# Linear attention in a mixer with experts: scores of two levels side by side in TensorE's order

## The chip, the cores and the metric

One core of a Trainium2 chip. The time is the device time of one execution in microseconds (us); several executions are run and their median is given. The profile shows one execution instruction by instruction. Its engines are TensorE (PE, with PEld for the loading of weights), VectorE (DVE), ScalarE (ACT), GpSimd (POOL) and SyncE (SP), which issues most DMAs.

## The reference

The layer takes x of 1024 tokens by 1024 features. It projects it by w_in into four HGRN heads of 128 and four GLA heads (keys of 64, values of 128), runs gated linear attention over each head, normalises each head, gates it, multiplies by w_out, and then goes through a layer norm, a hierarchical mixture of 64 experts (two a token) and another layer norm. The attention, cut to what matters:

```python
b = jnp.cumsum(lg, axis=3)                         # log decay
decay = jnp.exp(where(causal, b[t] - b[s], -inf))
scores = einsum('tk,sk->ts', q * decay, k)
o_intra = einsum('ts,sv->tv', scores, v)
S_next = exp(b_last) * S + einsum('sk,sv->kv', k * exp(b_last - b), v)
o = o_intra + einsum('tk,kv->tv', q * exp(b), S)
```

## The kernel before

The mixer runs until about 470 us of the profile; the experts follow. Everything of the mixer on TensorE is written in the order in which it shall run (`manual_schedule` for PE); for VectorE, ScalarE, GpSimd and SyncE a scheduler sets the order from the recorded program.

The work is cut into projections and six units. The projections (L174) multiply x with columns of w_in, in 48 matmuls a block (two halves of the tokens, eight slices of the features, three terms of a split of both factors into a high and a low part). `weights` loads a block's weights in two halves, ScalarE rounds them (L153) and VectorE takes the rest (L154). `fill(n)` issues the next n projections, `need(i)` those up to block i.

Units 0 to 3 are one HGRN head each (`nh = 1`), units 4 and 5 two GLA heads each (`nh = 2`). `gla(u, ...)` does a unit. The causal scores inside a chunk of 128 tokens are made in seven levels, li = 0 to 6: level 0 holds pairs of neighbours, level li the pairs between two blocks of 2^li. `level(li)` (L440) makes the scaled keys and queries: GpSimd subtracts decays (L462, L465), ScalarE takes the exponent (L463, L466), VectorE multiplies (L464 for keys Kb, L467 for queries Qb); for level 0 it is ScalarE twice (L451, L452) and VectorE four times (L453 to L456). There are two buffers each of Kb, Qb and d. `scores(li)` (L470) issues a burst of small matmuls into a PSUM bank, L477 for levels 0 to 4, L492 for 5, L504 for 6; levels 0 to 4 are then merged into `acc` by VectorE (`masked`, L428 and L431) and copied into A by GpSimd at level 4 (L484), levels 5 and 6 are copied into A by ScalarE (L497, L506). `banks` takes a bank of the pool "trp" for the first head, of "ou" for the second.

The loop over levels stands between projections: twelve of them before each burst (`n_lv`), at most one turn in front of a burst. Turns are transposes: those in `before` bring the output of the unit before into rows (L615, VectorE's copy L616), `turn_k` does the decayed keys (L538, ScalarE's copy L539). `decayed_k` and `decayed_q` make the keys and queries for the states.

Then the state phase of the unit: `state(0)` (L572, VectorE's copy L577), and for each of eight chunks the product of queries with the last state (L588), the product of A with values (L590), the next state (L572, VectorE L579), ScalarE's squares (L597), VectorE's copy (L598), and 12 projections (6 in unit 5). Among the chunks `prepare(u + 1)` runs: a logarithm (L379), one operation on k (L381), eight scans that make P, the running sum of the log decay (L400).

Of the kernel before, what the change touches and what calls it, by code (L numbers as in the profile page):

```python
# [9 lines left out]
F32 = mybir.dt.float32  # L10
# [10 lines left out]
NT = T // 128  # L21
# [35 lines left out]
def mixer_moe_kernel(ctx: ExitStack, tc: tile.TileContext, x_in, xT_in, wf_in, wv_in, wvg_in, wa2_in,  # L57
# [48 lines left out]
    ps_sc = ps_tr  # L106
# [89 lines left out]
    def fill(n):  # L196
        end = count[0] + n
        while count[0] < end and step():
            pass
# [204 lines left out]
    def gla(u, n_0, n_lv, n_ch, before, during):  # L404
# [26 lines left out]
                    V.copy_predicated(second(acc[:, hh], li), m.to_broadcast([128, NT, 16 >> li, 1 << li]),  # L431
                                      sps[hh].rearrange("p c (n h) -> p c n h", h=1 << li))

        def banks(shape):

            n = shape[0] * shape[1]
            return [(ps_sc.tile([128, 512], F32, name="trp") if hh == 0 else ps_ou.tile([128, 512], F32, name="ou"))
                    [:, :n].rearrange("p (c t) -> p c t", c=shape[0]) for hh in range(nh)]

        def level(li):  # L440
            h = 1 << li
            Kt, Qt = Kb[flip[0]], Qb[flip[0]]
            flip[0] ^= 1
            v4 = lambda a: a.rearrange("p (b two h) -> p b two h", two=2, h=max(h, 1))
            Kv, Qv, qv, kv, Pv = v4(Kt), v4(Qt), v4(q), v4(k), v4(P)

            if li == 0:
                lo_ = lg.rearrange("p (b two) -> p b two", two=2)[:, :, 1]
                e = g2.tile([128, T], F32, name="d")
                ep, em = e[:, :512, None], e[:, 512:, None]  # L450
                S.activation(ep[:, :, 0], lo_, AF.Exp, scale=0.5 * sc)  # L451
                S.activation(em[:, :, 0], lo_, AF.Exp, scale=-0.5 * sc)  # L452
                V.tensor_tensor(Qv[:, :, 0], qv[:, :, 0], em, OP.mult)  # L453
                V.tensor_tensor(Qv[:, :, 1], qv[:, :, 1], ep, OP.mult)
                V.tensor_tensor(Kv[:, :, 0], kv[:, :, 0], ep, OP.mult)
                V.tensor_tensor(Kv[:, :, 1], kv[:, :, 1], em, OP.mult)  # L456
            else:
                nb = T // (2 * h)
                e = g2.tile([128, T], F32, name="d")
                ev = v4(e)  # L460
                ref = Pv[:, :, 0, h - 1:h].to_broadcast([128, nb, h])
                G.tensor_tensor(ev[:, :, 0], ref, Pv[:, :, 0], OP.subtract)  # L462
                S.activation(ev[:, :, 0], ev[:, :, 0], AF.Exp, scale=sc)  # L463
                V.tensor_tensor(Kv[:, :, 0], kv[:, :, 0], ev[:, :, 0], OP.mult)  # L464
                G.tensor_tensor(ev[:, :, 1], Pv[:, :, 1], ref, OP.subtract)  # L465
                S.activation(ev[:, :, 1], ev[:, :, 1], AF.Exp, scale=sc)  # L466
                V.tensor_tensor(Qv[:, :, 1], qv[:, :, 1], ev[:, :, 1], OP.mult)  # L467
            return Kt, Qt

        def scores(li, Kt, Qt):  # L470
            if li < 5:
                sp = banks([NT, 16 if li else 32])
                for c in range(NT):
                    for hh in range(nh):
                        for j in range(4):
                            o = c * 128 + 32 * j
                            PE.matmul(sp[hh][32 * j:32 * j + 32, c], Kt[rows[hh], o:o + 32],  # L477
                                      second(Qt[rows[hh], None, o:o + 32], li)[:, 0], start=True, stop=True)
                masked(sp, li)
                if li == 4:  # L480
                    for hh in range(nh):
                        for j in range(4):
                            d_ = slice(32 * j, 32 * j + 32)
                            (G.tensor_copy if hh == 0 else S.copy)(A[hh][d_, :, d_], acc[d_, hh])  # L484
            elif li == 5:
                sp = banks([4, 32])
                for c in range(NT):
                    for hh in range(nh):
                        for b in range(2):
                            o = c * 128 + 64 * b  # L490
                            u_ = 64 * b + 32 * (c % 2)
                            PE.matmul(sp[hh][u_:u_ + 32, c // 2], Kt[rows[hh], o:o + 32],  # L492
                                      Qt[rows[hh], o + 32:o + 64], start=True, stop=True)
                for hh in range(nh):
                    for b in range(2):
                        for e in range(2):
                            S.copy(A[hh][64 * b:64 * b + 32, e::2, 64 * b + 32:64 * b + 64],  # L497
                                   sp[hh][64 * b + 32 * e:64 * b + 32 * e + 32])
            elif nh == 1:
                sp = ps_sc.tile([128, 4, 64], F32, name="trp")  # L500
                for c in range(NT):
                    o = c * 128
                    u_ = 64 * (c % 2)
                    PE.matmul(sp[u_:u_ + 64, c // 2], Kt[:, o:o + 64], Qt[:, o + 64:o + 128], start=True, stop=True)  # L504
                for e in range(2):
                    S.copy(A[0][0:64, e::2, 64:128], sp[64 * e:64 * e + 64])  # L506
            else:
                sp = banks([NT, 64])
                for c in range(NT):
                    o = c * 128  # L510
                    for hh in range(nh):
                        PE.matmul(sp[hh][rows[hh], c], Kt[rows[hh], o:o + 64], Qt[rows[hh], o + 64:o + 128], start=True,
                                  stop=True)
                for hh in range(nh):
                    S.copy(A[hh][0:64, :, 64:128], sp[hh][rows[hh]])
# [6 lines left out]
        def decayed_q():  # L522
            S.activation(QI, P, AF.Exp, scale=sc)
            V.tensor_copy(gdec, QI.rearrange("p (c i) -> p c i", i=128)[:, :, 127])
            V.tensor_tensor(QI, q, QI, OP.mult)

        def decayed_k():
            d = dd[0] = g1.tile([128, T], F32, name="lg")
            G.tensor_tensor(d.rearrange("p (c i) -> p c i", i=128), Pc[:, :, 127:128].to_broadcast([128, NT, 128]),
                            Pc, OP.subtract)  # L530
            S.activation(d, d, AF.Exp, scale=sc)
            V.tensor_tensor(d, k, d, OP.mult)

        def turn_k(half):
# [3 lines left out]
                PE.transpose(tp[:, i], dd[0][:, c * 128:(c + 1) * 128], ident)  # L538
            S.copy(KLt[:, half * 4:half * 4 + 4], tp)  # L539

        kqs = {0: level(0)}
        fill(n_0)
        for li in range(7):
            if li < 6:
                kqs[li + 1] = level(li + 1)
            if li == 2:
                decayed_k()
            if li == 3:
                decayed_q()
            fill(n_lv)  # L550
            if before and li > 1:
                before.pop(0)()
            if li in (5, 6):
                turn_k(li - 5)
            scores(li, *kqs.pop(li))
        fill(n_lv)


# [875 lines left out]
```

## Time and profile before

| | |
|---|---|
| runs | 1562.93, 1564.44, 1565.14 us, median 1564.44 us |
| profiled execution | 1563.61 us, its span 1561.8 us |
| busy share: PE, DVE, ACT, POOL | 92%, 45%, 29%, 25% |
| mean granted TensorE clock | 0.992 of full speed |

A row of the timeline gives the start and the length of an instruction (or of several alike), its engine, line, tiles and shapes; in brackets stands how long the engine was idle just before and what released it. Matmuls are pipelined: their ends are modelled, and the distance of starts tells the pace. The rows on which the prediction rests follow the change.

### The profile page before, as it was taken

To read this page: it belongs to the slowest core of one execution; us is meant where nothing else is said; L and a number is where in the kernel's file an instruction comes from. 1 tells how busy PE (TensorE), PEld (TensorE's weight loads), DVE (VectorE), ACT (ScalarE), POOL (GpSimd) and SP (SyncE) were. 2 spreads that over 40 slices of the span, in tenths; PEclk is the share of its full clock that TensorE was granted. 3 is DMA by queue.
4 is the path that set the end of the run, shared out by engine and by line. 5 is a ranking of instruction groups with operands and counts; after the bars stand their busy time and mean duration, and the time that the engine had idled before them with its cause. 6 is when DMAs were issued, how large, how long until landed. Compare 5 with 4: busy or idle time off the path is not lost. (4 is left out here: it accounts for less than half of the span.)

```text
span 1561.8 us, 23129 instructions
## 1 busy us (share of the span) xinstructions
PE 1437.8 (92%) x9359; PEld 800.1 (51%) x9359; DVE 707.6 (45%) x1719; ACT 451.1 (29%) x921; POOL 385.7 (25%) x281
## 2 busy tenths in 40 slices
PE   8899999899999999999998999999999899899895
PEld 5687787777788883333343333333344333334331
DVE  5666655647563783425234224223423333233224
ACT  5556555455531432121211111111121111111210
POOL 2524322423102211322212211321222122112211
PEclk9999999999999999999999999999999999999998
DMA  4111011100048349999999999999999999999992
GB/s 164 49 34 35 29 42 36 34 29 29 29 149 321 125 176 392 423 425 426 426 425 426 426 426 424 427 425 426 427 426 427 425 427 426 426 426 425 426 375 89
DMA packets 63311, 449.15 MB, mean 288 GB/s; under 512 B 12256, under 2 KB 20704, under 8 KB 38880
## 3 DMA queue, kind: packets, MB, share of 16 engines
q1 hardware_dynamic: 52032, 430.27, 66.4%
q0 software_dynamic: 9216, 12.61, 2.2%
q10 hardware_dynamic: 1952, 4.75, 0.8%
q8 instruction: 75, 1.23, 0.3%
q14 instruction: 36, 0.29, 0.1%
HBM read 447.58 MB, written 20.97 MB: 300 GB/s over the span
## 5 line engine op out<-in xcount | busy, mean ns | idle before, releaser
L1183 PE MATMUL gu<-w2u,VOA 128*64 128x512 f32 x992 | 338.9, 595 | 28.0 <-DMA w2u<-in_wg_dram 16.5
L1183 PE MATMUL gu<-w1u,VOA 128*64 128x512 f32 x1040 | 344.3, 595 | 15.0 <-DMA w1u<-in_wg_dram 14.9
L1183 PEld LDWEIGHTS gu<-w2u,VOA 128*64 128x64 f32 x992 | 101.7, 137 | 208.0 <-issue 154.2
L1045 ACT ACTIVATE VOA<-tp,cols 128x128 f32<-128x128 f32 x256 | 96.3, 457 | 337.0 <-PE tp L1042 336.7
L1032 POOL DMA_INDIRECT out_dram<-VOA,oidx x32 | 32.3, 1010 | 601.9 <-DVE VOA L1084 586.3
L1214 PE MATMUL yp<-w1u,hT 128*64 128x512 f32 x496 | 169.8, 599 | 12.1 <-DVE hT L1062 11.8
L1214 PE MATMUL yp<-w2u,hT 128*64 128x512 f32 x496 | 170.0, 598 | 11.7 <-DVE hT L1062 11.7
L1183 PEld LDWEIGHTS gu<-w1u,VOA 128*64 128x64 f32 x1040 | 106.5, 137 | 143.5 <-issue 108.8
L174 PE MATMUL pp<-xh,wh 128*128 128x512 f32 x416 | 172.9, 416 | 0.1
L174 PE MATMUL pp<-xh,wl 128*128 128x512 f32 x416 | 165.0, 397 | 1.9 <-DVE wl L154 1.9
L174 PE MATMUL pp<-xl,wh 128*128 128x512 f32 x416 | 166.4, 400 | 0.0
L1144 DVE SCALAR_TENSOR_TENSOR VOA<-VOA,cp 128x512 f32<-128x512 f32 x62 | 41.6, 682 | 268.7 <-PE cp L1135 263.4
L1069 DVE SCALAR_TENSOR_TENSOR y<-yp,gcol,y 128x512 fp32r<-128x512 f32 x64 | 47.9, 750 | 237.2 <-ACT y L1068 237.1
L1068 ACT ACTIVATE y<-yp,gcol 128x512 fp32r<-128x512 f32 x64 | 43.9, 687 | 211.2 <-PE yp L1214 208.7
L462 POOL TENSOR_TENSOR d<-P 128x512 f32<-128x512 f32 x36 | 51.3, 1425 | 177.9 <-DVE ny L88 65.3
L1189 ACT ACTIVATE sg<-gu 128x512 f32<-128x512 f32 x32 | 19.2, 599 | 250.6 <-PE gu L1183 250.6
L174 PEld LDWEIGHTS pp<-xh,wl 128*128 128x128 f32 x416 | 79.0, 190 | 19.7 <-DVE wl L154 2.8
L174 PEld LDWEIGHTS pp<-xh,wh 128*128 128x128 f32 x416 | 79.1, 190 | 18.7 <-issue 1.7
L1214 PEld LDWEIGHTS yp<-w1u,hT 128*64 128x64 f32 x496 | 49.0, 136 | 73.4 <-issue 55.3
L174 PEld LDWEIGHTS pp<-xl,wh 128*128 128x128 f32 x416 | 79.2, 190 | 13.8
L1214 PEld LDWEIGHTS yp<-w2u,hT 128*64 128x64 f32 x496 | 51.8, 136 | 63.7 <-issue 45.6
L1135 PE MATMUL cp<-y,same 128*128 128x512 f32 x304 | 78.8, 404 | 0.0
(294 smaller groups left out, 2138.8 us busy)
## 6 DMA issues: line engine op xcount, KB each, us to landing
w1u<-in_wg_dram SPq DMA_DIRECT2D x32, 2048.0 KB, 28.2
w2u<-in_wu_dram SPq DMA_DIRECT2D x31, 2048.0 KB, 30.8
w1u<-in_wu_dram SPq DMA_DIRECT2D x30, 2048.0 KB, 30.1
w2u<-in_wg_dram SPq DMA_DIRECT2D x30, 2048.0 KB, 28.0
w1u<-in_wd_dram SPq DMA_DIRECT2D x30, 2048.0 KB, 29.3
w2u<-in_wd_dram SPq DMA_DIRECT2D x30, 2048.0 KB, 29.5
wr<-in_wf_dram SPq DMA_DIRECT2D x36, 256.0 KB, 2.6
raw<-in_wout_dram SPq DMA_DIRECT2D x16, 256.0 KB, 5.1
```

What stands on the lines that cost most here:

```text
L174: PE.matmul(ps, w[:, k], x_[:, k, ts], start=(k == 0 and j == 0), stop=(k == KT - 1 and j == len(terms) - 1))
L462: G.tensor_tensor(ev[:, :, 0], ref, Pv[:, :, 0], OP.subtract)
L1032: return G.indirect_dma_start(out=dst, out_offset=bass.IndirectOffsetOnAxis(ap=idx, axis=0), in_=src, in_offset=None, bounds_check=rows - ...
L1045: S.activation(xt[:, c], tp[:, i], AF.Identity, bias=cols[:, 42 + c:43 + c], scale=cols[:, 34 + c:35 + c])
L1068: S.mul(yh[:, ns], yps[n], gate_col)
L1069: V.scalar_tensor_tensor(yl[:, ns], yps[n], gate_col, yh[:, ns], op0=OP.mult, op1=OP.subtract)
L1135: PE.matmul(cps[n], m, ys[q][:, i, n * 512:(n + 1) * 512], start=(first and j == 0 and i == 0), stop=(last and j == len(ms) - 1 and i == 1))
L1144: V.scalar_tensor_tensor(xg[:, ns], xg[:, ns], ALPHA, cps[n], op0=OP.mult, op1=OP.add)
L1183: PE.matmul(dst[64 * b:64 * b + 64], xt[:, c, 64 * b:64 * b + 64], utile[6 * p + u + b][:, c], start=(c == 0), stop=(c == KT - 1))
L1189: S.activation(sg, gp, AF.Silu)
L1214: PE.matmul(yps[n][64 * b:64 * b + 64], hT[:, c, 64 * b:64 * b + 64], utile[6 * p + 4 + b][:, c, n * 512:(n + 1) * 512], start=(c == 0), s ...
```

## The change

In the loop over levels, level 0 is still by itself; levels 1 and 2, 3 and 4, 5 and 6 are issued back to back, with 24 projections in front of each pair. Turns no longer stand in front of a burst: those of a pair are spread evenly among its 24 projections. The keys and queries of the two levels of the next pair are made right after a pair's scores are issued, followed by the decayed keys or the decayed queries. So that both bursts of a pair find a bank, in units with one head even levels now take a bank of "ou" and odd ones of "trp"; units with two heads use one of each for every level, as before. The number of projections and all other instructions of TensorE stay. Behind the changed lines the line numbers grow, first by 1, from the state phase on by 10.

```diff
--- before.py
+++ after.py
@@ -431,10 +431,11 @@
                     V.copy_predicated(second(acc[:, hh], li), m.to_broadcast([128, NT, 16 >> li, 1 << li]),
                                       sps[hh].rearrange("p c (n h) -> p c n h", h=1 << li))
 
-        def banks(shape):
+        def banks(shape, li):
 
             n = shape[0] * shape[1]
-            return [(ps_sc.tile([128, 512], F32, name="trp") if hh == 0 else ps_ou.tile([128, 512], F32, name="ou"))
+            trp = lambda hh: hh == 0 and (nh == 2 or li % 2)
+            return [(ps_sc.tile([128, 512], F32, name="trp") if trp(hh) else ps_ou.tile([128, 512], F32, name="ou"))
                     [:, :n].rearrange("p (c t) -> p c t", c=shape[0]) for hh in range(nh)]
 
         def level(li):
@@ -469,7 +470,7 @@
 
         def scores(li, Kt, Qt):
             if li < 5:
-                sp = banks([NT, 16 if li else 32])
+                sp = banks([NT, 16 if li else 32], li)
                 for c in range(NT):
                     for hh in range(nh):
                         for j in range(4):
@@ -483,7 +484,7 @@
                             d_ = slice(32 * j, 32 * j + 32)
                             (G.tensor_copy if hh == 0 else S.copy)(A[hh][d_, :, d_], acc[d_, hh])
             elif li == 5:
-                sp = banks([4, 32])
+                sp = banks([4, 32], li)
                 for c in range(NT):
                     for hh in range(nh):
                         for b in range(2):
@@ -497,7 +498,7 @@
                             S.copy(A[hh][64 * b:64 * b + 32, e::2, 64 * b + 32:64 * b + 64],
                                    sp[hh][64 * b + 32 * e:64 * b + 32 * e + 32])
             elif nh == 1:
-                sp = ps_sc.tile([128, 4, 64], F32, name="trp")
+                sp, = banks([4, 64], li)
                 for c in range(NT):
                     o = c * 128
                     u_ = 64 * (c % 2)
@@ -505,7 +506,7 @@
                 for e in range(2):
                     S.copy(A[0][0:64, e::2, 64:128], sp[64 * e:64 * e + 64])
             else:
-                sp = banks([NT, 64])
+                sp = banks([NT, 64], li)
                 for c in range(NT):
                     o = c * 128
                     for hh in range(nh):
@@ -538,21 +539,30 @@
                 PE.transpose(tp[:, i], dd[0][:, c * 128:(c + 1) * 128], ident)
             S.copy(KLt[:, half * 4:half * 4 + 4], tp)
 
+
         kqs = {0: level(0)}
         fill(n_0)
-        for li in range(7):
-            if li < 6:
-                kqs[li + 1] = level(li + 1)
-            if li == 2:
-                decayed_k()
-            if li == 3:
-                decayed_q()
-            fill(n_lv)
-            if before and li > 1:
-                before.pop(0)()
-            if li in (5, 6):
-                turn_k(li - 5)
-            scores(li, *kqs.pop(li))
+        kqs[1] = level(1)
+        fill(n_lv)
+        scores(0, *kqs.pop(0))
+        kqs[2] = level(2)
+        fill(2 * n_lv)
+        for li in (1, 3, 5):
+            if li > 1:
+                turns_ = [before.pop(0) for _ in range(2) if before]
+                if li == 5:
+                    turns_ += [lambda h=h: turn_k(h) for h in range(2)]
+                n = 2 * n_lv // (len(turns_) + 1)
+                for t_ in turns_:
+                    fill(n)
+                    t_()
+                fill(2 * n_lv - n * len(turns_))
+            for l_ in (li, li + 1):
+                scores(l_, *kqs.pop(l_))
+            if li < 5:
+                for l_ in (li + 2, li + 3):
+                    kqs[l_] = level(l_)
+                (decayed_k if li == 1 else decayed_q)()
         fill(n_lv)
```

The scheduler's order on the other engines moves too. VectorE, from unit 0 to unit 1, before (k, P and Kb, Qb are of unit 1, Sg the states of unit 0, osb its output, wl the rest of projection weights):

```order
L381 TENSOR_SCALAR k<-k 128x1024
L400 SCALAR_TENSOR_TENSOR P<-ones,lg 128x128 x8
L577 COPY Sg_117<-ou 128x128
L154 TENSOR_TENSOR wl<-wr,wh 128x512
L579 SCALAR_TENSOR_TENSOR Sg_118<-Sg_117,gdec,ou 128x128
L453 TENSOR_TENSOR Qb_114<-q,d 128x512
L454 TENSOR_TENSOR Qb_114<-q,d 128x512
L598 COPY osb<-ou 128x128
L455 TENSOR_TENSOR Kb_112<-k,d 128x512
```

And now:

```order
L381 TENSOR_SCALAR k<-k 128x1024
L400 SCALAR_TENSOR_TENSOR P<-ones,lg 128x128 x8
L456 TENSOR_TENSOR Kb_112<-k,d 128x512
L457 TENSOR_TENSOR Kb_112<-k,d 128x512
L465 TENSOR_TENSOR Kb_111<-k,d 128x256x2
L587 COPY Sg_117<-ou 128x128
L154 TENSOR_TENSOR wl<-wr,wh 128x512
L589 SCALAR_TENSOR_TENSOR Sg_118<-Sg_117,gdec,ou 128x128
L454 TENSOR_TENSOR Qb_114<-q,d 128x512
```

The three products of unit 1's keys, levels 0 and 1 (L456, L457, L465 of the changed kernel), come ahead of the copy of unit 0's first state (L587), which stood right behind the scans. From unit 1 to 2 it is the same.

ScalarE at the same place, before (KLt are the turned keys, Ab is A, lg the log decay of unit 1, d its exponents):

```order
L539 COPY KLt<-trp 128x512
L497 COPY Ab_115<-trp 32x4x32 x4
L539 COPY KLt<-trp 128x512
L379 ACT_TABLE_LOAD
L379 ACTIVATE lg<-k 128x1024
L506 COPY Ab_115<-trp 64x4x64 x2
L451 ACT_TABLE_LOAD
L451 ACTIVATE d<-lg 128x512
L452 ACTIVATE d<-lg 128x512
```

And now:

```order
L540 COPY KLt<-trp 128x512
L251 ACTIVATE q<-pp 128x512
L540 COPY KLt<-trp 128x512
L379 ACT_TABLE_LOAD
L379 ACTIVATE lg<-k 128x1024
L452 ACT_TABLE_LOAD
L452 ACTIVATE d<-lg 128x512
L453 ACTIVATE d<-lg 128x512
L498 COPY Ab_115<-trp 32x4x32 x4
L507 COPY Ab_115<-ou 64x4x64 x2
```

The table and the two exponents of unit 1's level 0 (L452, L453) come ahead of the six copies of levels 5 and 6 into A (L498, L507), of which four stood ahead of the second copy of the turned keys and two right behind the logarithm. From unit 1 to 2 it is the same.

## Rows read from the trace of the kernel before

**Rows 1.** Waits of TensorE, 40 to 480 us (line waited for: us in all, times, longest).

```profile
PE trp L477 <- DVE acc L431: 3.1, 1, 3.1
...
PE trp L492 <- DVE VOA L616: 1.7, 1, 1.7
PE trp L492 <- DVE acc L431: 1.6, 1, 1.6
PE trp L477 <- DVE acc L428: 1.3, 1, 1.3
```

**Rows 2.** Windows: busy us (x) of each engine, PEclk, DMA share, GB/s.

```profile
700.00:1561.00 861.00, 773.00 (x3303) 311.12 (x3299) 298.59 (x684) 139.94 (x307) 191.00 (x111) 0.99 0.97 409
```

**Rows 3.** Timeline of TensorE about scores 2 of unit 0 (start us, us).

```profile
61.80 0.39 PE L174 MATMUL pp<-xh,wl 128*128 128x512 f32 x1
62.12 0.73 PE L477 MATMUL trp<-Qb,Kb 128*32 128x16 f32 x64
62.78 0.50 PE L174 MATMUL pp<-xh,wh 128*128 128x512 f32 x1
63.12 0.39 PE L174 MATMUL pp<-xl,wh 128*128 128x512 f32 x1
```

**Rows 4.** Timeline of TensorE: a turn that stands alone.

```profile
55.43 0.60 PE L217 MATMUL trp<-cst,vt 128*128 128x128 f32 x4
55.78 0.48 PE L174 MATMUL pp<-xl,wh 128*128 128x512 f32 x1
```

**Rows 5.** Granted clock: two windows, and the matmuls with waits ahead of them.

```profile
339.20:346.00 6.80, 6.80 (x16) 4.90 (x17) 2.24 (x6) 6.01 (x9) 1.01 (x1) 0.50 0.20 69
...
390.40:393.90 3.50, 3.50 (x95) 2.89 (x84) 3.50 (x7) 1.26 (x2) 2.21 (x3) 0.51 0.02 5
...
339.14 1.12 PE L390 MATMUL pp<-gaT,wa 32*128 32x256 f32 x2 [1.13 <-DVE lg L392]
...
389.88 0.22 PE L477 MATMUL trp<-Qb,Kb 64*32 64x16 f32 x4 [3.13 <-DVE acc L431]
```

**Rows 6.** Timeline of TensorE, unit 1: second key turn, first state, chunk 1.

```profile
138.03 0.60 PE L538 MATMUL trp<-cst,lg 128*128 128x128 f32 x4
...
142.04 0.38 PE L572 MATMUL ou<-VOA,KLt 128*128 128x128 f32 x2
...
145.48 0.38 PE L588 MATMUL ou<-Sg,QI 128*128 128x128 f32 x2
```

**Rows 7.** Timeline of ScalarE, units 0 and 1: casts, copies into A, exponents.

```profile
73.53 0.60 ACT L153 CAST wh<-wr 128x512 fp32r<-128x512 f32 x1
...
75.65 1.06 ACT L497 COPY Ab<-trp 32x128 f32<-32x128 f32 x4 [0.55 <-PE trp L492]
...
139.27 1.28 ACT L379 ACT_TABLE_LOAD   x1
140.56 1.06 ACT L379 ACTIVATE lg<-k 128x1024 f32<-128x1024 f32 x1
141.53 0.74 ACT L506 COPY Ab<-trp 64x256 f32<-64x256 f32 x2
...
143.59 0.66 ACT L451 ACTIVATE d<-lg 128x512 f32<-128x512 f32 x1
```

**Rows 8.** Timeline of VectorE, unit 1: the scans of P.

```profile
142.27 2.62 DVE L400 TENSOR_TENSOR_SCAN P<-ones,lg 128x128 f32<-128x128 f32 x8
```

**Rows 9.** Timeline from unit 2 to 3: scans, POOL's subtraction, level 1 K.

```profile
201.61 2.63 DVE L400 TENSOR_TENSOR_SCAN P<-ones,lg 128x128 f32<-128x128 f32 x8
...
207.36 2.37 DVE L464 TENSOR_TENSOR Kb<-k,d 128x512 f32<-128x512 f32 x1 [1.94 <-ACT d L463]
...
206.28 1.04 POOL L465 TENSOR_TENSOR d<-P 128x512 f32<-128x512 f32 x1
```

**Rows 10.** Timeline of VectorE, unit 5: queries of level 2, a bank's read.

```profile
386.53 0.68 DVE L467 TENSOR_TENSOR Qb<-q,d 128x512 f32<-128x512 f32 x1
...
389.40 0.43 DVE L431 COPY_PREDICATED acc<-mski,trp 128x128 f32<-128x128 int32 x1
```

## The prediction

> **What bounds the kernel now.** I read the mixer first, because the change touches nothing else. The waits of TensorE between 40 and 480 us are few [rows 1]: apart from four of them at the scores of unit 0 and unit 5, TensorE is fed. So in the mixer the end is set by TensorE's own instructions plus those waits. The late part is another thing: from 700 us on the DMA engines are busy for 0.97 of the time [rows 2], so nothing gained there would come from TensorE. But its loads of expert weights go into tiles that the mixer uses until its end, so I take a shift of the mixer's end as a shift of the kernel's end, one to one.
>
> The sum is made against the profiled execution, 1563.61 us, which lies 0.8 us below the median of the three runs, 1564.44 us. I take 0.2% (3.1 us) as what a measurement of this kernel can tell from no change.
>
> **The change part by part.**
>
> *Merged bursts.* Projections follow each other at 0.23 us. Around one burst of scores the projections at 61.80 and 62.78 stand 0.98 us apart and the next one comes 0.34 later [rows 3]: the burst costs 0.75 + 0.11 = 0.86 us. Of that 0.09 is entry (the projections' pace would have it start at 62.03) and 0.11 the slow first projection; the exit behind the last of the 64 pieces I put at 0.1, an estimate by the entry. So about 0.3 us a burst is not its own matmuls. Before, each unit has seven bursts; now four (level 0, and three pairs): 3 x 6 units x 0.3 = **-5.4 us**. It may be nothing, if the second level of a pair pays the same entry; the bounds are 0 and -5.4. I take -5.4, because the 64 pieces of one burst, in several places of the array, stand in one row of the trace, with no idle time between them.
> The step from level 5 to level 6 alone changes the shape (32 columns, then 64). The Trainium skill, "TensorEngine Tiling (Array Packing)", section Key Properties, says that changing the tiling mode drains TensorE, which speaks against that third pair. The entry of 62.12, 0.09 us later than the projections' pace [rows 3], is in agreement with it; by this rule six of the pairs would pay 0.09 again and the sum would be 0.5 us less.
>
> *Turns.* Turns of keys and of the last unit's output move from before a score to among the projections. One among projections takes 0.35 us [rows 4], and a slow projection behind it (0.1 by rows 3) that a burst has anyway when the turn stands beside it. At most 0.1 each is lost, for the four turns of a unit some 0.4, 2 us over the mixer (the bound); one beside a burst pays an entry between its 128 columns and the burst's 32 instead, so I take 0. TensorE makes the same matmuls, and SP's and POOL's instructions keep their order. ACT loads two tables fewer; they lie beside projections, so 0.
>
> *Unit 0.* Scores 1 and 5 wait 1.3 and 1.6 us [rows 1], because their one kind of bank is still read by VectorE. Level 2 now goes to the other pool and every pair comes 24 projections (5.5 us) after the last, so both waits go. The keys of levels 3 to 6 are made later than before; I put 0.2 us for one that is just late (bounds 0 and 0.7): **-2.7 us**.
>
> *Unit 5.* Scores 2 wait 3.1 us and scores 5 wait 1.7 [rows 1]. In both, VectorE stood before them in a queue (a wide normalisation, and only then, at 389.40, the read of the level 1 bank [rows 10]; for scores 5 the copy of a turn). Level 1 and 2 now use banks of both pools that level 0 has long left, so the first goes; turns lie 5 projections or more ahead of the pair, so the second goes. What is late next: the queries of level 2 end at 387.2 [rows 10], while the pair falls due at about 386.4 (389.88 less the wait of 3.13 [rows 5], less a turn that stood before it), so 0.8 us; and the copies of the two turns now stand behind the queries of level 4, about 0.5 to 1 us at the next scores and at the key turn. Gone 4.8, new 1.8: **-3.0 us** (bounds -4.8 and 0).
>
> *The clock.* The granted clock fell to 0.51 from 390.4 to 393.9, behind the wait of 3.13 us, and to 0.50 from 339.2 to 346, behind one of 1.13 us [rows 5]. At that level (1.2 GHz) 16 matmuls filled 6.8 us, 0.43 us apart, so a stretch costs its length times (1 - 0.23/0.43): 1.6 us and 3.1 us. The stretch at 390 loses the wait ahead of it: **-1.5 us** (bounds 0 and -1.6). The one at 339 stays.
>
> *New waits at the state phase of units 0 and 1.* VectorE's order shows it: after the scans of P it now makes three K tiles of the next unit (level 0 twice, level 1) ahead of the copy of the first state; and ScalarE makes the next unit's two exponents ahead of its six copies into A. Before, neither was so. TensorE's chunk 0 needs A, chunk 1 needs that state, and behind chunk 1 every projection waits. Call the start of the first state S0.
> First ScalarE. In unit 1 the second key turn is at 138.03, S0 at 142.04, and the scans end at 144.89 [rows 6, 8]: 6.86 after the turn. The turn now lies 8 projections further ahead and the level 5 burst (0.4) between: S0 comes 4.01 + 1.84 + 0.4 + 0.1 = 6.3 after it (0.4 is an estimate for 32 pieces, half those of rows 3 and twice as wide; 0.1 the turn's own slow projection), so the scans end at about S0 + 0.5. The logarithm ends 3.27 before them [rows 7], S0 - 2.7; then one table (1.28), two exponents (0.66 each), four copies (1.06) and two (0.74) [rows 7]: A is ready at S0 + 1.6, while chunk 0 is due at S0 + 0.2, behind one matmul of the state. Wait 1.4 us. In unit 0 the key copies stand behind a weight cast (73.53 before [rows 7]) that a DMA bounds, and I put 1.3 more, an estimate: 2.7 us.
> Then VectorE. From the scans' end to the level 1 K: at the least POOL 1.04, exponent 0.66, product 0.68 and 0.24 of hand-over, 2.6 us. From unit 2 to 3, where the program before already has this order, from 204.24 to 209.73, 5.5 us [rows 9]; there TensorE had projections to do until 208, so nobody waited. With the copy, 2.9 to 5.8 us after the scans. Chunk 1 is due at S0 + 3.44 [rows 6]. Unit 1: S0 + 3.4 to 6.3, a wait of 0 to 2.9, but at least 1.4 from chunk 0. Unit 0 (scans end at S0 + 1.8): 1.3 to 4.2, at least 2.7. Together 4.1 to 7.1. No row is nearer than the analog, which is the upper end, but there POOL's subtractions ran beside other products than here; I take the middle, **+5.6 us**.
> What makes the analog long is the product of 207.36, 2.37 us beside POOL's next subtraction, against 0.68 for one by itself [rows 9, 10]. The Trainium skill, "SBUF — State Buffer", section SBUF: two separate sides, calls the shared port pair of VectorE and GpSimd an exclusive lock, the loser blocked for the whole instruction; by that rule the K product always waits for POOL's wide subtraction, the long price holds, this term is +7.1 and the sum -5.5. The row of 2.37 agrees with it.
>
> Units 2, 3 and 4 gain the merged bursts alone; their first state comes after further projections, or VectorE's order there is as before.
>
> Sum: -5.4 - 2.7 - 3.0 - 1.5 + 5.6 = -7.0 us, 1556.6 against the profiled execution, and 0.8 more against the median: **1557.4 us**. The rivals' times below stand against the median too.
>
> **Rivals.**
> 1. *The pairs save nothing* (each level pays its own entry, the gain is gone wherever bursts lie). For it: no two bursts lie together in the trace of before. Against: the 64 pieces of one burst run without gaps. The sum is then -1.6, 1562.8 us. The scores would lie together, and it would be worth nothing.
> 2. *More*: the K products come early (4.1) and neither unit 0 nor unit 5 takes a new wait at its scores (-2.9, -4.8): -5.4 - 2.9 - 4.8 - 1.5 + 4.1 = -10.5, 1553.9 us. For it: a product by itself is 0.68. Against: the analog of 5.5 us.
> 3. *Slower, by the clock*: the new waits in the state phase are each followed by half clock, as the wait of 1.13 at 339 was [rows 5]. Place: units 0 and 1, 3.1 us each (6.3), and in unit 5 the stretch stays and one of 1.6 joins it; with the full price of the waits -5.4 - 2.7 - 3.0 + 7.1 + 6.3 + 1.6 = +3.9, 1568.3 us. It decides from the point where more than one long stretch comes: without them 4.0 us are left, and 3.1 is one. For it: new waits are as long as the one at 339. Against: of the five waits of rows 1 and 339 only two were followed by a fall, and those of 1.3, 1.6 and 1.7 us were not.
>
> **How the numbers follow.** The forecast has 0.50, rival 1 0.20, rival 2 0.17, rival 3 0.13. The forecast's own range is 1554.5 to 1561 by its bounds. The 8 in 10 take in rivals 1 and 2 and leave out 3: 1552.8 to 1564.5. Faster by over 3.1 us: nearly all of the forecast (0.46), rival 2, a little of rival 1 (0.03): 0.66. Within: 0.22. Slower: 0.12, rival 3 with little else.
>
> **What would show it.** Right: the first scores of level 2 start right behind those of level 1, without an entry; no wait over 1 us at a score in unit 0; new waits of TensorE in the state phase at chunk 0 (on ScalarE's copy into A) and chunk 1 (on the copy of the first state), 2.5 to 4 us in unit 0 and 1.3 to 3 in unit 1; full clock around 390. Wrong: a score pair with an entry between its levels; half clock after the new waits; waits of more than 2 us at the scores of units 1 to 4, which this sum doesn't have; or an end of the mixer that moves without the end of the kernel.

## The result and the profile after

The changed kernel takes 1572.01 us (median of 6 runs, 1571.51 to 1577.65), the kernel before 1564.79 us in the same measurement: ratio 1.0057, 95% interval 1.0043 to 1.0071. It is slower, by 7.2 us; 1557.4 was predicted, with a range to 1564.5. The profiled execution took 1572.11 us, span 1570.2 us.

First the waits of TensorE between 40 and 480 us, the view of [rows 1] (line waited for: us in all, times, longest). Kernel after:

```profile
PE ou L600 <- ACT Ab L507: 4.2, 2, 2.1
PE ou L598 <- DVE Sg L587: 3.2, 2, 1.6
PE ou L598 <- DVE Sg L589: 3.2, 1, 3.2
PE trp L478 <- issue: 2.3, 1, 2.3
PE pp L174 <- issue: 2.2, 1, 2.2
...
PE trp L478 <- DVE ny L88: 1.5, 1, 1.5
PE trp L478 <- DVE VOA L626: 1.4, 1, 1.4
...
PE ou L478 <- issue: 0.5, 1, 0.5
```

The four waits of [rows 1] are gone. In their place stand the two kinds that the prediction added at the state phase (on A, L507, in units 0 and 1; on the first state, L587, in units 0 and 2), waits at scores of units 4 and 5 (L626, L88), and a kind that it didn't have: "issue", 5 us in which TensorE waited for nothing that the profile shows. (The wait on L589, 3.2 us in unit 3, is old.)

Then the granted clock, the view of [rows 5], in five windows of the kernel after:

```profile
144.70:148.10 3.40, 3.40 (x10) 2.45 (x8) 2.34 (x2) 3.23 (x5) 2.88 (x3) 0.50 0.00 0
291.50:298.30 6.80, 6.19 (x20) 5.22 (x21) 2.84 (x8) 2.88 (x8) 2.29 (x2) 0.50 0.12 36
329.10:332.40 3.30, 3.17 (x24) 2.55 (x24) 1.76 (x5) 0.65 (x2) 0.20 (x1) 0.50 0.10 23
346.20:349.50 3.30, 3.30 (x8) 2.57 (x9) 1.50 (x4) 3.28 (x6) 0.00 (x0) 0.50 0.01 2
393.90:400.70 6.80, 4.65 (x13) 3.77 (x14) 5.96 (x9) 2.11 (x4) 4.88 (x4) 0.50 0.01 2
```

Half clock (1.2 GHz) holds for 23.6 us of the mixer, against 10.3 in the two windows of [rows 5]. By the price of the prediction, 0.46 us a us, 13.3 us more cost up to 6 us, an estimate: it holds where TensorE has work, and in part of the last window it waited anyway (busy 4.65 of 6.80).

Five instructions that every version has date the loss: one in the state phase of each of units 0, 1, 3 and 4, and one behind unit 5. Timeline of TensorE, kernel before:

```profile
96.17 0.33 PE L217 MATMUL trp<-cst,vt 128*128 128x128 f32 x1 [0.97 <-ACT vt L212]
155.84 0.33 PE L217 MATMUL trp<-cst,vt 128*128 128x128 f32 x1 [1.03 <-ACT vt L212]
268.56 0.48 PE L390 MATMUL pp<-gaT,wa 32*128 32x256 f32 x1 [0.64 <-DVE lg L392]
...
441.70 0.33 PE L615 MATMUL trp<-cst,osb 128*128 128x128 f32 x1 [0.31 <-DVE osb L609]
```

Kernel after:

```profile
95.81 0.33 PE L217 MATMUL trp<-cst,vt 128*128 128x128 f32 x1 [0.43 <-ACT vt L212]
158.32 0.33 PE L217 MATMUL trp<-cst,vt 128*128 128x128 f32 x1 [0.42 <-ACT vt L212]
271.03 0.48 PE L390 MATMUL pp<-gaT,wa 32*128 32x256 f32 x1 [0.64 <-DVE lg L392]
345.40 0.48 PE L390 MATMUL pp<-gaT,wa 32*128 32x256 f32 x1 [1.13 <-DVE lg L392]
448.27 0.33 PE L625 MATMUL trp<-cst,osb 128*128 128x128 f32 x1 [0.31 <-DVE osb L619]
```

With 339.14 of [rows 5] for the fourth, the differences are -0.4, +2.5, +2.5, +6.3 and +6.6 us: nothing lost in unit 0, 2.8 us to the mark of unit 1, nothing to that of unit 3, 3.8 us to that of unit 4, 0.3 to the end of unit 5, and 1.8 more behind the mixer (span 1561.8 to 1570.2). A shift of the mixer did reach the end: in all fourteen profiles of this study the span ends 1120.1 to 1123.7 us behind the last mark. Of the 3.8 us to the mark of unit 4, some 3 (an estimate by the same price) are the window at 291.50. It begins in a wait of 3.2 us that the kernel before has too, there without half clock.

### The profile page after: what moved, and what is told of

The parts are those of the page before. It is cut to its first block, busy times and chain, and to the rows that moved or that the text cites. A ratio compares the mean times of both kernels' runs of the same rounds, so it can differ in the third digit from the quotient of the medians.

```text
span 1570.2 us, 23136 instructions
## 1 busy us (share of the span) xinstructions
PE 1440.4 (92%) x9359; PEld 805.1 (51%) x9359; DVE 706.7 (45%) x1719; ACT 449.7 (29%) x919; POOL 389.9 (25%) x281
## 3 DMA queue, kind: packets, MB, share of 16 engines
q8 instruction: 75, 1.23, 0.3%
```

## The experiments

Three causes were to be told apart: the state phase's order, the units with two heads, and the pairs themselves. "Loop of before" below means the old loop over levels for the units named. The same five marks in each run, as read from TensorE's timelines (us), the median, and the interval of the ratio to the kernel before as it ran beside each. Marks and waits are those of one profiled execution, the median is of 4 to 10; where the two lie apart (the profiled one is 4.3 us above the median in e12, 1.5 to 1.7 in e1, e5, e7 and e11), the marks show more loss than the median:

| run | unit 0 | unit 1 | unit 3 | unit 4 | unit 5 | median | against before (95%) |
|---|---|---|---|---|---|---|---|
| before | 96.17 | 155.84 | 268.56 | 339.14 | 441.70 | 1564.79 | |
| after | 95.81 | 158.32 | 271.03 | 345.40 | 448.27 | 1572.01 | 1.0043 to 1.0071 |
| e1 no third pair | 93.25 | 152.38 | 264.11 | 338.16 | 445.06 | 1567.49 | 1.0002 to 1.0026 |
| e2 old loop in units 4, 5 | 95.69 | 158.32 | 271.02 | 341.86 | 443.07 | 1567.09 | 1.0011 to 1.0030 |
| e3 both | 93.47 | 152.56 | 264.30 | 334.63 | 435.98 | **1559.40** | 0.9955 to 0.9978 |
| e4 turns ahead of the pair | 95.11 | 162.47 | 277.68 | 354.32 | 458.51 | 1582.25 | 1.0095 to 1.0133 |
| e5 gap inside pairs | 93.30 | 152.40 | 264.12 | 336.99 | 439.82 | 1562.15 | 0.9971 to 0.9992 |
| e6 early key turns alone | 98.25 | 162.65 | 275.24 | 346.53 | 447.40 | 1570.79 | 1.0030 to 1.0058 |
| e7 third pair, late key turns | 95.08 | 158.51 | 272.69 | 343.24 | 444.80 | 1566.00 | 0.9997 to 1.0018 |
| e8 turns from level 3 | 93.16 | 152.25 | 263.97 | 336.33 | 438.99 | 1561.61 | 0.9976 to 0.9995 |
| e9 scores repeated | 93.28 | 152.89 | 272.70 | 344.02 | 445.10 | 1568.41 | 1.0023 to 1.0046 |
| e10 banks alone | 93.02 | 152.69 | 265.50 | 336.19 | 437.95 | 1562.16 | 0.9966 to 0.9993 |
| e11 pairs, old banks | 94.40 | 153.48 | 266.75 | 339.13 | 440.47 | 1561.89 | 0.9974 to 0.9997 |
| e12 unit 5 spaced | 93.49 | 152.59 | 264.32 | 337.33 | 439.14 | 1560.40 | 0.9952 to 0.9985 |

### The third pair and the units with two heads (e1, e2, e3)

e1 takes levels 5 and 6 apart again:

```diff
-for li in (1, 3, 5):
+for li in (1, 3):
...
+for li in (5, 6):
+    fill(n_lv)
+    if before:
+        before.pop(0)()
+    turn_k(li - 5)
+    scores(li, *kqs.pop(li))
 fill(n_lv)
```

> Levels 5 and 6 are issued apart again, each behind 12 projections with a key turn in front, as before the change; pairs 1+2 and 3+4 stay. Theory (the loss of units 0 to 2 is the other engines' order at the state phase, which the early key turns bring): the waits at chunk 0 on A (2.1 us in units 0 and 1) and at chunk 1 on the first state (1.6 in units 0 and 2), and the half clock at 144.7, go; six third pairs less cost some 1.5 us; about 7 us less than the changed kernel, 1564 to 1566. Rival (a pair itself costs, a third of the loss for each kind of pair): about 1569.6, and the state-phase waits stay.

The waits on A and on the first state of units 0 to 2 are gone, as the theory had it: at the mark of unit 3 the run is 4.5 us ahead of the kernel before, where the changed one was 2.5 behind: seven us. But at the last mark it is 3.4 behind: from there on, through the units with two heads, it loses 7.8 us. The median, 1567.49, lies between the two expectations, and the marks show why: the waits of the state phase went whole, and the loss of the units with two heads became larger.

e2 keeps the new loop for units 0 to 3 alone (both loops made functions):

```diff
+        (new_loop if u < 4 else old_loop)()
```

> Units 4 and 5 (two heads) take the loop of before, units 0 to 3 the new one. Theory: the loss of units 4 and 5 (2.6 us at the last projection: bank waits, two stalls of 2.2 us without a releaser, half clock at 329 and 394) goes, the state-phase waits of units 0 to 2 stay: about 1569.4. Rival (all of the loss comes from the state phase, whose low clocks only shift into units 4 and 5): 1572, with the half clock elsewhere.

1567.09: units 4 and 5 no longer lose, and the state-phase waits stay. It also shows what the half clock hid. In the kernel after, unit 1 waits at chunk 0 (2.08 us) and then runs 3.4 us at half clock, and is not late at chunk 1; here the clock stays up and chunk 1 waits 1.61 us. Both are at 158.32 at the mark. Here the half-clock stretch took the place of the wait and did not add to it. Timeline of TensorE in e2:

```profile
143.40 0.46 PE L621 MATMUL ou<-VOA,Ab 128*128 128x128 f32 x2 [2.21 <-ACT Ab L507]
148.48 0.46 PE L619 MATMUL ou<-Sg,QI 128*128 128x128 f32 x2 [1.61 <-DVE Sg L608]
```

e3 has both edits.

> Both of the two edits: units 0 to 3 with pairs 1+2 and 3+4 alone, units 4 and 5 as before. Theory: the causes are separate and add up; unit 0 keeps the gain of its two score waits (2.9), eight pairs give 0.25 each: 4 to 5 us faster than the kernel before, about 1560. Rival (pairs give nothing and the two waits come back elsewhere): 1564, no difference.

1559.40 us: without the third pair, and with the old loop in the units with two heads, the idea is a gain, 0.9966 of the kernel before (0.9955 to 0.9978). This is the fastest version of the study, by its median. The two edits do not simply add up, as was expected: alone they give 4.5 and 4.9 us, together 12.6; by the marks the difference arises in the units with two heads, where e1 lost more than the kernel after. By the marks e3 gains 2.7 us to unit 0's, 0.6 to unit 1's and 1.0 to unit 3's.

### What turns the order over: the key turns (e4, e6, e7)

e6 starts from e3 and only moves the key turns of units 0 to 3, 8 projections ahead of their scores (`before` is empty there, so its two lines drop out):

```diff
-    fill(n_lv)
-    if before:
-        before.pop(0)()
-    turn_k(li - 5)
+    fill(n_lv - 8)
+    turn_k(li - 5)
+    fill(8)
     scores(li, *kqs.pop(li))
```

> As the run with pairs 1+2 and 3+4 in units 0 to 3 alone, but each key turn stands 8 projections ahead of its score instead of right in front of it; no third pair. Theory (early key turns bring the next unit's work forward on ScalarE and VectorE): the waits at chunk 0 and chunk 1 of units 0 and 1 come back, 0.7 to 2 us each, and with them half clock in one place or two: 1563 to 1567. Rival (it takes the third pair to make these waits): no difference to that run, 1559.4.

The order did turn over as in the kernel after (three K products ahead of the first state's copy), with no third pair. Waits of TensorE in e6:

```profile
PE ou L624 <- DVE Sg L613: 6.4, 3, 2.7
...
PE ou L624 <- DVE Sg L615: 3.2, 1, 3.2
PE ou L626 <- ACT Ab L507: 1.9, 2, 1.0
```

Unit 0 loses 4.8 us against e3, unit 1 another 5.3. So the turns' place is enough to bring these waits back; the loss was larger than expected (1570.79, not 1563 to 1567). The waits at chunk 1 are 2.7 us in units 0 and 1, against 1.6 in the kernel after, and half clock followed in both.

e4 leaves all three pairs and puts each pair's turns in front of it:

```diff
-    n = 2 * n_lv // (len(turns_) + 1)
-    for t_ in turns_:
-        fill(n)
-        t_()
-    fill(2 * n_lv - n * len(turns_))
+    fill(2 * n_lv)
+    for t_ in turns_:
+        t_()
```

> All three pairs stay; the turns of a pair stand together right in front of it, behind its 24 projections. Theory: the waits on A in units 0 and 1 go (the copies stand before the exponents again), and most of the wait on the first state; but in units 4 and 5 each pair needs both banks of trp right behind two turns, whose copies take 0.75 us each: 1.5 to 3 us lost in each of these. 1566 to 1570. Rival (spreading the turns is harmless): no difference to the changed kernel, 1572.

10 us slower than the changed kernel, worse than either expectation. The waits on A went and 0.4 us of the wait on the first state is left, but scores now wait for copies of turns in units 1 to 5 (six us in five places), and values of the next unit come late (L217, 3.4 us at the longest); half clock holds for 37.5 us. So turns in a block right ahead of a pair are 10 us worse than spread ones. With e6, the fault of the spreading is where it puts the key turns.

e7 does e3 with the third pair, key turns late:

```diff
-    if li == 5:
-        turns_ += [lambda h=h: turn_k(h) for h in range(2)]
...
+    if li == 5:
+        for h in range(2):
+            turn_k(h)
     for l_ in (li, li + 1):
```

> As the same run, with the third pair in units 0 to 3 and both key turns right in front of it, the other turns spread. Theory (the third pair costs nothing itself, and saves 0.3 us a unit): no waits on A, 1558 to 1559. Rival (levels 5 and 6 together are late for the copies into A, whatever the turns do): a wait of 1 to 2 us at chunk 0 in units 0 and 1, 1562 to 1565.

Neither was right. No wait on A, as the theory had it; yet 1566.00. The loss lies elsewhere, in the copy of projected values (L212) on ScalarE. Waits of TensorE in e7, and timeline of ScalarE ahead of the longer one:

```profile
PE trp L217 <- ACT vt L212: 7.4, 4, 3.4
```

```profile
154.57 0.64 ACT L467 ACTIVATE d<-d 128x512 f32<-128x512 f32 x1 [0.80 <-POOL d L466]
157.35 0.63 ACT L464 ACTIVATE d<-d 128x512 f32<-128x512 f32 x1 [2.14 <-POOL d L463]
157.89 0.57 ACT L212 COPY vt<-pp 128x512 f32<-128x512 f32 x1
```

The copy stands behind an exponent of unit 2 that waits 2.1 us for GpSimd; in e3 the copy starts at 151.93. A third pair brings the four copies of level 5 to where those of level 6 already stood; that this is what makes ScalarE and GpSimd late there is argued, not shown.

### The waits with no releaser: TensorE's own instructions (e5, e9, e8)

In the kernel after, unit 5 stands still twice with "issue" as the releaser, 2.19 us behind the pair 1+2 and 2.25 in the middle of the pair 3+4. Nothing in the program waits there. Timeline of TensorE:

```profile
396.05 0.79 PE L174 MATMUL pp<-xh,wh 128*128 128x512 f32 x1 [2.19 <-issue]
...
409.20 0.22 PE L478 MATMUL trp<-Qb,Kb 64*32 64x16 f32 x4 [2.25 <-issue]
```

In a unit with two heads a pair is 256 small matmuls, each with its own weight load: 512 instructions. The page's section of DMA queues has a queue "instruction" (q8) with 75 packets and 1.23 MB, 16 KB each. DMA view, windows 393.6 to 394.8 and 406.4 to 407.7 us:

```profile
q8 instruction: 1, 0.02, 5.0%
...
q8 instruction: 1, 0.02, 5.4%
```

One such packet lands while TensorE stands, and it goes on 1.3 to 1.5 us behind the window's end. That is a coincidence until it is made on purpose. e9 starts from e3 and repeats score matmuls in one-head units, where no data is late:

```diff
-                for c in range(NT):
+                times = {(1, 1): 2, (2, 1): 4}.get((u, li), 1)
+                for c in list(range(NT)) * times:
```

> As the run with pairs 1+2 and 3+4 in units 0 to 3 alone, with the scores of level 1 issued twice in unit 1 and four times in unit 2 (same operands, same bank). No wait on data is added. Theory (fetch): in unit 2, 256 pieces with 256 weight loads and the 64 of level 2 behind them stall TensorE for about 2 us, with no releaser, and one fetch of TensorE's instruction queue ends just ahead of where it goes on; in unit 1, 128 + 64 pieces, none or under 0.5. 0.56 us of matmuls a repeat is 2.2, so 1563 to 1565. Rival (tiny matmuls issue at their own pace for as long as there are any): no stall, 1561.6.

Timeline of TensorE in e9, unit 2, levels 1 (trp) and 2 (ou), and the DMA view for 178.8 to 180.2 and 182.3 to 183.5 us:

```profile
177.60 1.64 PE L479 MATMUL trp<-Qb,Kb 128*32 128x16 f32 x172
181.30 0.86 PE L479 MATMUL trp<-Qb,Kb 128*32 128x16 f32 x82 [2.06 <-issue]
181.99 0.20 PE L479 MATMUL ou<-Qb,Kb 128*32 128x16 f32 x1
181.99 0.19 PE L479 MATMUL trp<-Qb,Kb 128*32 128x16 f32 x1
182.01 0.22 PE L479 MATMUL ou<-Qb,Kb 128*32 128x16 f32 x1
182.01 0.21 PE L479 MATMUL trp<-Qb,Kb 128*32 128x16 f32 x1
182.03 0.79 PE L479 MATMUL ou<-Qb,Kb 128*32 128x16 f32 x42
184.75 0.51 PE L479 MATMUL ou<-Qb,Kb 128*32 128x16 f32 x20 [1.94 <-issue]
```

```profile
q8 instruction: 1, 0.02, 5.1%
...
q8 instruction: 1, 0.02, 5.0%
```

Between the two stalls are exactly 128 pieces (82 + 1 + 1 + 1 + 1 + 42), with their weight loads 256 instructions: one packet of 16 KB, which makes 64 bytes each. Two stalls came where one was expected, 4.0 us, and 7 us of half clock from the first one on; 1568.41, more than 1563 to 1565. In unit 1 (192 pieces at once) there was none.

Two counts through the traces settle what the packets are. The 256 pieces that e9 adds are 512 instructions with their weight loads, and its page has 77 packets, two more. And of the waits with "issue" over 0.35 us in the mixer there are 24, in twelve of the fourteen versions (e3 and e10 have none). Counted from the program's start, each of the 24 ends at TensorE instruction 256 n + 193 or 194, when n packets have landed. From the start of that last packet to where TensorE goes on are 2.3 to 2.7 us each time, while 128 pieces with their loads take 1.2 us (172 in 1.64). TensorE outruns the fetch of its own program, in steps of 256 instructions. Where a stall comes thus depends on where in the program the small matmuls lie, too, and not on their number alone.

e5 has e1 with 6 projections between the two levels of a pair in units 4 and 5, taken from those ahead of the pair:

```diff
-    fill(2 * n_lv - n * len(turns_))
+    fill(2 * n_lv - n * len(turns_) - (6 if nh == 2 else 0))
-    for l_ in (li, li + 1):
-        scores(l_, *kqs.pop(l_))
+    scores(li, *kqs.pop(li))
+    if nh == 2:
+        fill(6)
+    scores(li + 1, *kqs.pop(li + 1))
```

> As the run without the third pair, with 6 projections between the two levels of a pair in units 4 and 5, so that 128 pieces stand together there and not 256. Theory (256 pieces with their 256 weight loads outrun the fetch of TensorE's instructions): the stalls without a releaser in units 4 and 5 (0.4, 2.5 and 3.1 us there) go or fall under 0.5, and unit 5 loses 5 us less, with one half-clock stretch less perhaps: 1560 to 1563. Rival (the two levels wait for a bank or a tile which the profile doesn't name): the stalls stay, 1567.

1562.15, as the theory had it, 5.3 us less than e1: of the three "issue" stalls of e1 (2.5, 3.1 and 0.4 us) the largest fell to 0.4; but one of 2.2 stays behind level 2 of unit 5, and that of unit 4 grew to 1.1. Six projections are not enough everywhere.

e8 is e3 with turns from level 3 on in units 4 and 5:

```diff
-                if before and li > 1:
+                if before and li > 2:
```

> As the same run, units 4 and 5 with turns of the unit before from level 3 on instead of 2, so that scores 2 find a bank that level 0 has left. Theory (the wait of 3.3 us at scores 2 of unit 5 is for the bank, not for the tiles): it goes, with the half clock behind it: 1554 to 1557. Rival (the wait moves to the next scores or turns): 1558 to 1560.

1561.61: the bank was what scores 2 of unit 5 waited for (3.3 us in e3), and that wait is gone; but 1.4 us for the queries came in its place (the profile names L88, which stands right behind their product), and then 2.5 us of "issue", 3.9 in all. Timeline of TensorE in e8:

```profile
387.42 0.58 PE L174 MATMUL pp<-xh,wh 128*128 128x512 f32 x1 [2.48 <-issue]
```

No pair stands there: two bursts of 128 pieces with 12 projections between do it too. So the wait of 3.13 us in the kernel before, at 389.88 [rows 5], and that of 3.3 in e3, lay over a fetch: there the packet lands within the wait (387.37 to 388.33 in the kernel before), and no stall follows. That is why the large wait of unit 5 could be taken away and give nothing.

### Banks and pairs apart (e10, e11), and a try at unit 5 (e12)

e10 has the loop of before in every unit, and the change's `banks`.

> The loop of before in every unit, with the change's banks alone (one-head units: even levels in ou, odd in trp). Theory: the two waits at unit 0's scores (1.3 and 1.6 us) are for banks and go, nothing else moves: 1561.5. Rival (it is the longer distance between pairs that takes them away): 1564, the waits stay.

1562.16, and unit 0 ends 3.2 us earlier: both waits were for banks. Units 1 to 4 gain nothing by it.

e11 has e3 with `trp = lambda hh: hh == 0`, the banks of before.

> As the run with pairs 1+2 and 3+4 in units 0 to 3 alone, with the banks of before (all levels of a one-head unit in trp). Theory (pairs need the second pool): the second level of a pair, or the turn behind it, waits for a bank, 0.3 to 1.5 us in each of four units: 1561 to 1565. Rival (two banks of trp are enough for a pair): 1559.4.

1561.89: pairs do wait for banks then (1.3 and 0.5 us in unit 0, 1.0 and 0.3 in unit 3), and units 1 and 2 do not. e3 is 2.5 us better than this, and 2.8 better than e10. Against the kernel before, the banks alone give 2.5 us, the pairs alone 2.7, and both 5.1: by the medians they add up. The interval of each is some 2 us either way, and those of e3 and e10 overlap.

e12 gives unit 5 of e3 other distances:

```diff
-                fill(n_lv)
+                fill({0: 6, 1: 14, 2: 22, 3: 12, 4: 10, 5: 10, 6: 10}[li] if u == 5 else n_lv)
```

> As the run with pairs 1+2 and 3+4 in units 0 to 3 alone (1559.4), with the bursts of unit 5 behind 6, 14, 22, 12, 10, 10 and 10 projections instead of 12 each, so that scores 1 come 0.9 us earlier and scores 2 1.4 us later. Theory (the wait of 3.3 us at scores 2 is what VectorE's queue and the instruction fetch both need after scores 1, and projections in front cover it): the wait falls to 1 to 2 us, 1557 to 1558.5. Rival (the time comes back at the later bursts, which stand closer): 1559 to 1560.

No gain that can be measured (1560.40, runs from 1556.25 to 1565.95). The wait of 3.3 us fell to three of 1.2, 0.6 and 1.0 us, the last with no releaser; the sum is about as long. The profiled execution, 1564.73, has 20.5 us of half clock in the mixer, against 10.2 in e3's, so it says little of the median. e12 can't be told from e3.

## Why the prediction was wrong, step by step

The forecast of -7.0 us failed in four terms. Unit 5 was put at -3.0, and its waits grew by 1.1. The clock was put at -1.5, and half clock cost up to 6 more. Unit 4 was to gain its merged bursts alone, and took waits of 1.4 us more. The state phase was put at +5.6, and took 7.4. These differences make some 15 us; the profiled execution, 1572.11, lies 15.5 us above the 1556.6 of the sum. That they agree so well is partly luck: waits and half clock overlap, and more than half of the -5.4 us was never measured by itself.

- **Merged bursts: right for two pairs of a one-head unit; the other ten of 18 bursts are not shown.** Timeline of TensorE in e3, the first pair of unit 1:

```profile
126.53 0.39 PE L174 MATMUL pp<-xh,wl 128*128 128x512 f32 x1
126.84 0.70 PE L478 MATMUL trp<-Qb,Kb 128*32 128x16 f32 x62
...
127.41 0.75 PE L478 MATMUL ou<-Qb,Kb 128*32 128x16 f32 x62
128.09 0.50 PE L174 MATMUL pp<-xh,wh 128*128 128x512 f32 x1
128.43 0.40 PE L174 MATMUL pp<-xl,wh 128*128 128x512 f32 x1
```

  The second level starts in the pace of the first. From 126.53 to 128.09 are 1.56 us, then 0.34 to the next projection; less 0.23 each that is 1.44 us, against 2 x 0.86 by [rows 3]: 0.28 saved, 0.3 predicted. By the marks of e3, unit 1 gains 0.6 us by its two pairs, and units 2 and 3 together 1.0. The -5.4 took in six third pairs and four pairs in units 4 and 5 as well, ten of the 18 bursts that it saves. No run shows their gain by itself: e7, with third pairs in units 0 to 3, and e1, with pairs in units 4 and 5, are slower than e3. By the rule in the Trainium skill, "TensorEngine Tiling (Array Packing)", section Key Properties, level 6 behind level 5 would pay a drain. In the kernel after level 6 starts 0.38 us behind level 5, where 32 pieces took 0.46 with the modelled end; no entry of 0.09 can be read from that.
- **Unit 0: right.** Its waits were for banks (e10: 3.2 us), and they went.
- **New waits of the state phase: right place in units 0 and 1, unit 2 missed.** The steps hold one by one in unit 0. Timeline of VectorE, kernel after:

```profile
77.50 2.62 DVE L400 TENSOR_TENSOR_SCAN P<-ones,lg 128x128 f32<-128x128 f32 x8
80.04 0.66 DVE L456 TENSOR_TENSOR Kb<-k,d 128x512 f32<-128x512 f32 x1
...
83.24 2.37 DVE L465 TENSOR_TENSOR Kb<-k,d 128x512 f32<-128x512 f32 x1 [1.93 <-ACT d L464]
85.53 0.28 DVE L587 COPY Sg<-ou 128x128 f32<-128x128 f32 x1
```

  S0 is at 78.39, the scans end at 80.12, S0 + 1.7 (predicted 1.8); the K product of level 1 ends 5.5 us later, the analog of [rows 9] to a tenth. Waits 2.10 and 1.64, 3.7 us against 2.7 to 4.2. Unit 1 waits 3.8 us in e2, where 1.4 to 2.9 was predicted, and unit 2 waits 1.5 us that the sum did not have: VectorE's order there is that of before, where I said nobody would wait. In the kernel before that was so by nothing to spare: the copy of the first state (L577) ended at 211.72, and chunk 1 began at 211.78. ScalarE now makes the four copies of level 5 just ahead of the logarithm from which the scans come, and the projections that had covered the rest no longer do. Altogether 7.4 us of waits against +5.6, just over the bound of 7.1. The Trainium skill, "SBUF — State Buffer", section SBUF: two separate sides, gave the long price by its exclusive lock; the row of 2.37 us in unit 0 agrees, beside 0.68 for a product by itself [rows 10].
- **Unit 5: wrong, and this is a step that failed.** "What is late next" was read from VectorE's queue alone: 1.8 us, a gain of 3.0. In its place came 1.5 us on the queries and 4.4 us with no releaser, so that 4.8 us of waits became 6.0. The prediction took TensorE's instructions as always there; pieces come at some 0.01 us each, and the fetch of 256 instructions takes longer than their work (2.3 us and more against 1.2). A row of the kernel before did hint at it: its waits hold one "issue" of 0.4 us in unit 4, which was read over.
- **Unit 4: missed.** Scores 3 and 4 of a two-head unit need both banks of trp, and two turns stand just ahead that use the same two; the second's copy (L626) stands on VectorE behind a weight rest (L154) that a cast is late for. TensorE waited 1.35 us, and half clock came behind it. Timeline, kernel after:

```profile
326.21 0.69 DVE L154 TENSOR_TENSOR wl<-wr,wh 128x512 fp32r<-128x512 f32 x1 [3.16 <-ACT wh L153]
326.82 0.74 DVE L626 TENSOR_SCALAR VOA<-trp,cols 128x512 f32<-128x512 f32 x1
327.61 0.22 PE L478 MATMUL trp<-Qb,Kb 64*32 64x16 f32 x4 [1.35 <-DVE VOA L626]
```
- **The clock: wrong in sign.** -1.5 us was forecast for a fall that would go with its wait; 13 us more of half clock came. Rival 3 was this, at 1568.3 with a chance of 0.13: its mechanism (each new wait can bring a half-clock stretch) was right. It placed the stretches in units 0, 1 and 5; they fell in units 1, 3, 4 and 5, and its sum lacks unit 4 and the fetch. The wait of 3.2 us in unit 3 goes with none in the kernel before and with 6.8 us in the kernel after. The chance of 0.13 was too low: of five waits that I counted two had been followed by a fall, and I added four or more new ones while I took none to be.
- **TensorE fed apart from four waits: read too narrowly.** The view of [rows 1] has further waits in the kernel before, of up to 3.2 us. The longest is that in unit 3, during which half clock began in the kernel after:

```profile
PE ou L588 <- DVE Sg L579: 3.2, 1, 3.2
```

Rival 1 (pairs save nothing) fell. In rival 2 units 0 and 5 without new waits fell too.

## What to carry to other kernels

When a table of work on one engine moves, read the other engines' order at the next place where that engine has no slack: here a turn 8 projections earlier let the scheduler put the next unit's products ahead of a 0.3 us copy on which everything waited, and that cost more than the merged bursts gave. Before a long wait is counted as a gain, ask what it has been covering, the fetch of the instructions too: 512 tiny instructions together stalled TensorE for 2 to 3 us at seven of twelve places (kernel after, e1, e4). And apply such an edit per kind of unit: the same loop, less its third pair and with its banks, gains 5 us in the units with one head (e3), and in those with two it costs 8 (e1 against e3).

## What the hardware showed unexpectedly

- TensorE's program comes in packets of 16 KB, 256 instructions; small matmuls at some 0.01 us each (172 in 1.64 us) use one up faster than the next comes, and TensorE stands for up to 3.1 us with no releaser in the profile. 192 pieces at once passed without a stall in unit 1 of e9; 320 stalled twice in unit 2; of the four pairs of 256 in the kernel after, both of unit 5 stalled for 2.2 us, one of unit 4 for 0.5 and one not.
- In the kernel after, half clock fell behind waits of 1.35 and 2.08 us, and not behind others of 1.64 and 2.10; versions whose programs agree up to a place differ in it there (unit 1 of the kernel after and of e2). Of the 7.2 us up to some 6 hang on it, and its runs spread over 6 us; so a version of this kernel is to be judged by its waits as well as by its time.
